# The merges' small products in halves and the queries' norm products in quarters, each part behind a dense tile

## The chip, the core and the metric

One core of one Trainium2 chip runs the whole program. The metric is the device time of one execution in microseconds (us). TensorE is called PE, VectorE DVE, ScalarE ACT, GpSimd POOL, and SyncE SP; SP issues nearly all the loads.

## What is computed

Two blocks on 256 tokens of 1024 features, in float32. The first is a layer with four branches. The second adds 16 meta tokens, runs a mixer and then a mixture of experts. The change lies in the mixer:

```python
def hybrid_mixer(h, norm_g, w_in, conv_w, a_log_f, dt_bias_f, a_log_b, dt_bias_b,
                 out_norm_g, w_fourier, w_delta, w_out):
    hn = rms_norm_2(h, norm_g)
    proj = hn @ w_in
    f_in, qkv, z, ab, gate_f, gate_d = jnp.split(proj, points, axis=-1)
    f_mix = jnp.real(jnp.fft.fft2(fg, axes=(1, 3), norm="ortho")).astype(h.dtype)
    y_f = f_mix.reshape(bsz, seq_len, F_WIDTH) @ w_fourier
    qkv = jax.nn.silu(depthwise_conv_centred(qkv, conv_w))
    q, k, v = jnp.split(qkv, [QK_WIDTH, 2 * QK_WIDTH], axis=-1)
    q = l2_normalize(...) * (HEAD_DK ** -0.5)
    ...
    o_fwd = gated_delta_chunked(qp, kp, vp, pad_to_chunks(g_f), pad_to_chunks(beta_f))
    o_bwd = flip(gated_delta_chunked(flip(qp), ...))
    o = rms_norm_2(o, out_norm_g) * jax.nn.silu(zf)
    y_d = o.reshape(bsz, seq_len, V_WIDTH).astype(h.dtype) @ w_delta
    merged = jax.nn.sigmoid(gate_f) * y_f + jax.nn.sigmoid(gate_d) * y_d
    return merged @ w_out
```

`gated_delta_chunked` solves a unit lower triangular system in each chunk and then scans over the chunks with a state of 128 by 128 for each of 8 heads. The mixture of experts picks one of 8 groups and two of its 8 experts for each token; the kernel reads the weights of all 64 experts, 192 loads of 1 MB, named `wexp`.

## The kernel before

**Dense tiles.** A projection is done in tiles of 128 output features. `load` (L269) has SP fetch the weight tile (`wraw`, L283), ACT writes its high part (`whi`, L293), and POOL or DVE subtracts to get the low part (`wlo`, L300; POOL in two halves). `dense_fm` (L333) then issues 24 PE products per tile: high part by high and low part of the tokens (L340, L341), 8 each, and low part by high part (L345), 8. They have 256 or 272 columns. The tiles of the second block stand in a queue in the order of their weights: among the last are `wf` (the input projections, which the queue takes from first), `wfo` (Fourier output, products with `fhl`), `wde` (delta output) and `wo`.

**Chains woven between dense tiles.** The latency-bound work is written as generators: at each `yield`, `weave` (L973) lets `fill` issue dense tiles, W4 = 1.0 per step for `merges`, W5 = 2.6 per step for `q_factors` and the two scans. The generators' instructions have a raised priority. A list scheduler then fixes the order in which each engine runs its instructions; PE runs what it was given in that order and waits where an operand is not there. So an edit to a generator can move everything behind it.

**merges** (L1455) puts the inverses of 32 diagonal blocks together, from 32 to 64 to 128. First ACT, DVE and POOL copy blocks (L1465, L1467, L1469). `Zp` (L1475) is 64 products of 32 by 32, copied by ACT to `Zs` (L1479); `Wp` (L1485, L1486) is 128 such products. Then `Z2` (L1501) and `W2` (L1511, L1513), two groups of 16 products of 64 by 64 each, with ACT's copies `Z2s` (L1503) between. The two `Z2` and the two `W2` tiles read as `Z` and `W` in the trace.

**q_factors** (L1522) squares the queries on ACT and sums the squares by 16 PE products with one column each (`psrq`, L1529). **scan** (L1546) runs for two directions and two chunks: `psks`, `psqs`, `psvn`, `psS`, and last `pso` (L1605), which DVE adds to the output (`dec`, L1610). When both directions have added theirs, **output_norm** (L1618) squares and sums that output (L1629, L1630), takes a reciprocal root in small DVE steps, scales the output (L1644) and transposes it on PE (`psoT`, L1648). Then `on` (L1671), `hTh` (L1672) and `hTl` (L1674) make the operand of the `wde` tiles; the expert phase comes after those, the output projection and the router.

**Expert loads.** 24 slots hold expert chunks ahead of their use; SP issues the loads into them between the loads of dense tiles. A float32 product shows in the trace as two records.

Of the kernel before, what the change touches and what calls it, by code (L numbers as in the profile page):

```python
# [22 lines left out]
L = NM + S  # L23
# [9 lines left out]
NU = 2  # L33
# [184 lines left out]
def body(ctx, tc, A, out, dbg=None, stage=9):  # L218
    nc = tc.nc
    kit = Kit(tc)  # L220
    V, SC, G, PE = nc.vector, nc.scalar, nc.gpsimd, nc.tensor
# [22 lines left out]
    ones = cp.tile([P, 128], F32, name="ones")  # L244
# [88 lines left out]
    def dense_fm(jobs, x, c0, c1, nk):  # L333

        xh, xl = x
        g = dict(skip_group_check=True) if len(jobs) > 1 else {}
        for j, (ps, (wh, wl), o) in enumerate(jobs):
            for k in range(nk):
                ks = slice(o + k * P, o + k * P + P)
                PE.matmul(ps, wh[:, ks], part(xh, k, slice(c0, c1)), start=j + k == 0, stop=False, **g)  # L340
                PE.matmul(ps, wh[:, ks], part(xl, k, slice(c0, c1)), start=False, stop=False, **g)  # L341
        for j, (ps, (wh, wl), o) in enumerate(jobs):
            for k in range(nk):
                ks = slice(o + k * P, o + k * P + P)
                last = PE.matmul(ps, wl[:, ks], part(xh, k, slice(c0, c1)), start=False, stop=k == nk - 1, **g)  # L345
        return last
# [61 lines left out]
    with ExitStack() as b1:  # L408
# [67 lines left out]
        hT = feature_major(S)  # L476
# [31 lines left out]
        for j in range(4):  # L508
            wst["hi"] = HI0[j]
            w = load(A["wtok"][j], 8 * CH, 2) if j else w0  # L510
# [21 lines left out]
            for t in range(2):  # L532
                ps, rt = pss[t], r1[:, t:t + 1]
# [27 lines left out]
        evac, done = [], []  # L561
# [326 lines left out]
    with b2:  # L888
# [55 lines left out]
        for n in SEQ2:  # L944
            base2[n] = o_
            o_ += (COL2[n][1] - COL2[n][0]) // P
        queue, nload = [], [NU]

        def fill(n=1):
            for _ in range(n):  # L950
# [35 lines left out]
        def dense(n, a, c0, use):  # L986
            def go(w):
                ps = kbig[a] if n == "k" and a in KBIG else bank("psd")
                dense_fm([(ps[:, c0:L], w[0], 0)], hT, c0, L, 8)
                use(a, ps[:, c0:L])  # L990
            queue.append([n, lambda: load_tiles(A["wf2"], base2[n] + a, 1, D), go, None])

# [462 lines left out]
        def merges():  # L1455
# [13 lines left out]
                G.tensor_copy(OTf[bs, :, 32 * (b % 2):32 * (b % 2) + 32],  # L1469
                              src[bs, :, 16 * f:16 * f + 16].rearrange("p c a -> p a c"))  # L1470
            Zp = x32(big("Zp"))
            for a in range(32):
                for p2 in range(2):
                    r0, c0 = 64 * p2, 64 * p2 + 32
                    PE.matmul(Zp[c0:c0 + 32, a], Anf[r0:r0 + 32, a, c0:c0 + 32], Xc[r0:r0 + 32, :, a], start=True, stop=True)  # L1475
            Zs = x32(big_c("Zs"))
            for p2 in range(2):
                c0 = 64 * p2 + 32
                SC.activation(Zs[c0:c0 + 32], Zp[c0:c0 + 32], AF.Copy)  # L1479
            yield  # L1480
            Wp = x32(big("Wp"))
            for a in range(32):
                for p2 in range(2):
                    r0, c0 = 64 * p2, 64 * p2 + 32
                    PE.matmul(Wp[r0:r0 + 32, a], Zs[c0:c0 + 32, a], Xr[c0:c0 + 32, :, a], start=True, stop=True)  # L1485
                    PE.matmul(Wp[c0:c0 + 32, a], Xr[c0:c0 + 32, :, a], Zs[c0:c0 + 32, a], start=True, stop=True)  # L1486
            SC.activation(OTf[32:64, :, 0:32], Wp[32:64, F_], AF.Copy)
            V.tensor_copy(Vff[64:96, F_, 96:128], Wp[64:96, F_])
            SC.activation(Vff[0:32, F_, 32:64], Wp[0:32, F_], AF.Copy)
# [32 lines left out]
        def q_factors():  # L1522
            ps = bank("psrq")
            for t in range(2):
                qsq = big_c("qsq")
                for i, half in enumerate(halves("q")):
                    SC.activation(qsq[:, 4 * i:4 * i + 4], half[:, :, NM + t * P:NM + t * P + P], AF.Square)
                for h in range(8):
                    PE.matmul(ps[:, 8 * t + h:8 * t + h + 1], qsq[:, h], ones[:, 0:1], start=True, stop=True)  # L1529
                yield  # L1530
            V.tensor_scalar(rq, l2(ps[:, :16], 16, "q"), 128 ** -0.5, None, op0=ALU.mult)
            V.tensor_tensor(rq2, rq, rq, op=ALU.mult)

# [525 lines left out]
```

## Time and profile before

| | |
|---|---|
| median of 3 runs | 1168.31 us (1164.94 to 1168.77) |
| profiled execution | 1169.51 us |
| its span | 1167.7 us |
| mean granted TensorE clock | 0.934 |
| PE busy | 1051.7 us, 90% |
| DVE, ACT, POOL busy | 549.8, 440.5, 424.6 us |
| DMA | 307.71 MB, mean 264 GB/s; 420 GB/s in the expert phase |

The span is the profiled execution from its first to its last instruction; the 1.8 us beside it are start and end. "PEclk" is the share of full clock that PE was granted: 1.00 is 2.4 GHz and 0.50 is 1.2 GHz, and a value between is a window that holds both. Busy shares tell which engine works, not which one the end waits for; that is read from what ended the idle time and from the order of the work on PE.

### The profile page before, as it was taken

To read this page: it belongs to the slowest core of one execution; us is meant where nothing else is said; L and a number is where in the kernel's file an instruction comes from. 1 tells how busy PE (TensorE), PEld (TensorE's weight loads), DVE (VectorE), ACT (ScalarE), POOL (GpSimd) and SP (SyncE) were. 2 spreads that over 40 slices of the span, in tenths; PEclk is the share of its full clock that TensorE was granted. 3 is DMA by queue.
4 is the path that set the end of the run, shared out by engine and by line. 5 is a ranking of instruction groups with operands and counts; after the bars stand their busy time and mean duration, and the time that the engine had idled before them with its cause. 6 is when DMAs were issued, how large, how long until landed. Compare 5 with 4: busy or idle time off the path is not lost. (4 is left out here: it accounts for less than half of the span.)

```text
span 1167.7 us, 21453 instructions
## 1 busy us (share of the span) xinstructions
PE 1051.7 (90%) x8798; PEld 849.2 (73%) x8798; DVE 549.8 (47%) x1202; ACT 440.5 (38%) x753; POOL 424.6 (36%) x348
## 2 busy tenths in 40 slices
PE   7999999999998979899999999999977777888794
PEld 7999999999998879799999997455443333443351
DVE  5947754433446798887356874222221111111112
ACT  5546453444457554556323553112111111111112
POOL 4565433567773684869455651000000000000100
PEclk9999998999999989999889999999998898777888
DMA  8554532555554432354228798999999999999994
GB/s 319 178 181 147 179 123 95 196 178 204 181 181 139 148 109 73 109 175 164 74 73 312 288 349 322 408 420 420 420 421 421 420 420 420 421 420 421 420 420 171
DMA packets 58859, 307.71 MB, mean 264 GB/s; under 512 B 5984, under 2 KB 7264, under 8 KB 33280
## 3 DMA queue, kind: packets, MB, share of 16 engines
q1 hardware_dynamic: 56528, 301.59, 66.5%
q10 hardware_dynamic: 2224, 4.65, 1.1%
q8 instruction: 72, 1.18, 0.4%
q14 instruction: 35, 0.29, 0.1%
HBM read 304.12 MB, written 2.10 MB: 262 GB/s over the span
## 5 line engine op out<-in xcount | busy, mean ns | idle before, releaser
L300 POOL TENSOR_TENSOR wlo<-wraw,whi 128x512 fp32r<-128x512 f32 x230 | 322.0, 1424 | 210.0 <-ACT whi L293 135.1
L340 PE MATMUL psd<-hTh,whi 128*128 128x256 f32 (+2 forms) x1096 | 276.8, 289 | 1.4 <-DVE vr L1039 0.6
L341 PE MATMUL psd<-hTl,whi 128*128 128x256 f32 (+2 forms) x1096 | 275.2, 288 | 2.6 <-DVE hTl L458 2.6
L293 ACT ACTIVATE whi<-wraw 128x1024 fp32r<-128x1024 f32 (+1 forms) x183 | 193.8, 1064 | 192.2 <-PE psd L341 143.8
L341 PEld LDWEIGHTS psd<-hTl,whi 128*128 128x128 f32 x1096 | 211.3, 193 | 4.6 <-DVE hTl L458 3.5
L340 PEld LDWEIGHTS psd<-hTh,whi 128*128 128x128 f32 x1096 | 211.6, 193 | 3.8 <-issue 1.5
L1808 PE MATMUL psgu<-wexp,xg 128*32 128x512 f32 x1024 | 146.1, 659 | 39.6 <-DMA wexp<-in_wex_dram 39.4
L345 PE MATMUL psd<-hTh,wlo 128*128 128x256 f32 (+2 forms) x1096 | 157.7, 288 | 0.0
L1996 POOL TENSOR_SCALAR wexp<-cst,gcol 128x128 f32<-128x128 f32 x8 | 4.7, 603 | 389.1 <-PE psgu L1808 389.1
L300 DVE TENSOR_TENSOR wlo<-wraw,whi 128x1024 fp32r<-128x1024 f32 (+1 forms) x68 | 100.9, 1488 | 92.2 <-PE psd L345 52.2
L345 PEld LDWEIGHTS psd<-hTh,wlo 128*128 128x128 f32 x1096 | 143.2, 193 | 1.2 <-issue 1.0
L1808 PEld LDWEIGHTS psgu<-wexp,xg 128*32 128x32 f32 x1024 | 24.8, 112 | 113.2 <-DMA wexp<-in_wex_dram 84.7
L1794 PEld LDWEIGHTS psg<-pm,x 128*128 128x128 f32 x512 | 76.4, 231 | 17.4 <-issue 12.9
L1847 PE MATMUL psy<-wexp,at 128*32 128x256 f32 x1024 | 78.8, 416 | 11.1 <-DVE at L1837 9.2
L1794 PE MATMUL psg<-pm,x 128*128 128x128 f32 x512 | 84.4, 322 | 0.0
L1856 DVE SCALAR_TENSOR_TENSOR yl<-psy,ww,yh 128x256 fp32r<-128x256 f32 x64 | 31.0, 484 | 102.2 <-ACT yh L1855 97.1
L1855 ACT ACTIVATE yh<-psy,ww 128x256 fp32r<-128x256 f32 x64 | 30.3, 474 | 127.4 <-PE psy L1847 121.9
L1814 DVE SCALAR_TENSOR_TENSOR act<-act,psgu 128x256 f32<-128x256 f32 x16 | 6.7, 422 | 132.1 <-ACT act L1813 132.1
L1813 ACT ACTIVATE act<-psgu 128x256 f32<-128x256 f32 x16 | 6.1, 384 | 135.9 <-PE psgu L1808 135.9
L1847 PEld LDWEIGHTS psy<-wexp,at 128*32 128x32 f32 x1024 | 29.6, 114 | 36.9 <-DVE at L1837 13.4
L1796 DVE TENSOR_SCALAR xg<-psg,gcol 128x128 f32<-128x128 f32 x64 | 22.4, 350 | 62.5 <-ACT xg L1795 61.7
L1795 ACT ACTIVATE xg<-psg,gcol 128x128 f32<-128x128 f32 x64 | 23.5, 368 | 71.3 <-PE psg L1794 71.3
(646 smaller groups left out, 1640.1 us busy)
## 6 DMA issues: line engine op xcount, KB each, us to landing
wexp<-in_wex_dram SPq DMA_DIRECT2D x191, 1024.0 KB, 19.8
wraw<-in_wf_dram SPq DMA_DIRECT2D x39, 1024.0 KB, 4.9
wraw<-in_wf_dram SPq DMA_DIRECT2D x53, 512.0 KB, 4.4
wraw<-in_wbr_dram SPq DMA_DIRECT2D x8, 1024.0 KB, 5.2
wraw<-in_wtok_dram SPq DMA_DIRECT2D x4, 1160.0 KB, 8.5
wraw<-in_wout_dram SPq DMA_DIRECT2D x4, 1024.0 KB, 4.7
wraw<-in_wde_dram SPq DMA_DIRECT2D x8, 512.0 KB, 6.2
wraw<-in_wo_dram SPq DMA_DIRECT2D x8, 512.0 KB, 7.2
```

The costliest lines, as they stand in the source:

```text
L293: SC.activation(hi, rs, AF.Copy)
L300: eng.tensor_tensor(lo[:, h], rs[:, h], hi[:, h].bitcast(F32), op=ALU.subtract)
L340: PE.matmul(ps, wh[:, ks], part(xh, k, slice(c0, c1)), start=j + k == 0, stop=False, **g)
L341: PE.matmul(ps, wh[:, ks], part(xl, k, slice(c0, c1)), start=False, stop=False, **g)
L345: last = PE.matmul(ps, wl[:, ks], part(xh, k, slice(c0, c1)), start=False, stop=k == nk - 1, **g)
L1794: PE.matmul(ps[:, f], hn[:, t, fs], self.pm[:, t].rearrange("p e c -> p (e c)"), start=t == 0, stop=t == 1)
L1795: SC.activation(self.xg[:, 2 * f2], ps[:, 0], AF.Copy, scale=gcol[:, 3, 2 * f2:2 * f2 + 1])
L1796: V.tensor_scalar(self.xg[:, 2 * f2 + 1], ps[:, 1], gcol[:, 3, 2 * f2 + 1:2 * f2 + 2], None, op0=ALU.mult)
L1808: PE.matmul(gu[32 * q:32 * q + 32, :], self.xg[:, k, 32 * q:32 * q + 32], ws[k][:, 512 * q:512 * q + 512], start=k == 0, stop=k == 7)
L1847: PE.matmul(self.ps[32 * q:32 * q + 32, cs], self.at[:, k, 32 * q:32 * q + 32], self.ws[8 + c][:, o:o + 256], start=k == 0, stop=k == 1)
L1855: SC.activation(yh, self.ps[:, cs], AF.Copy, scale=self.ww)
L1856: V.scalar_tensor_tensor(yl, self.ps[:, cs], self.ww, yh.bitcast(F32), op0=ALU.mult, op1=ALU.subtract)
```

## The change

`done[0]` keeps the last PE product of the dense tile issued last. `behind_dense()` ties the PE instructions in its block behind that product in PE's order. The `Zp` products, the `Wp` products and each chunk's `psrq` products are split in two, with a `yield` between the parts, so that `weave` issues a dense tile there. The number of instructions is the same.

```diff
-        queue, nload = [], [NU]
+        queue, nload, done = [], [NU], [None]
+
+        def behind_dense():
+
+            return tc.issue_after(done[0].ins)
...
-                dense_fm([(ps[:, c0:L], w[0], 0)], hT, c0, L, 8)
+                done[0] = dense_fm([(ps[:, c0:L], w[0], 0)], hT, c0, L, 8)
...
             Zp = x32(big("Zp"))
-            for a in range(32):
-                for p2 in range(2):
-                    r0, c0 = 64 * p2, 64 * p2 + 32
-                    PE.matmul(Zp[c0:c0 + 32, a], ...)
+            for half in range(2):
+                with behind_dense():
+                    for a in range(16 * half, 16 * half + 16):
+                        for p2 in range(2):
+                            r0, c0 = 64 * p2, 64 * p2 + 32
+                            PE.matmul(Zp[c0:c0 + 32, a], ...)
+                if not half:
+                    yield
...
             Wp = x32(big("Wp"))
-            for a in range(32):
+            for half in range(2):
+                with behind_dense():
+                    for a in range(16 * half, 16 * half + 16):
...
+                if not half:
+                    yield
...
-                for h in range(8):
-                    PE.matmul(ps[:, 8 * t + h:8 * t + h + 1], qsq[:, h], ones[:, 0:1], start=True, stop=True)
-                yield
+                for h0 in (0, 4):
+                    with behind_dense():
+                        for h in range(h0, h0 + 4):
+                            PE.matmul(ps[:, 8 * t + h:8 * t + h + 1], qsq[:, h], ones[:, 0:1], start=True, stop=True)
+                    yield
```

**At the first merge, on PE.** The rows are an engine's instructions in order: line, operation, output and inputs, shape, count. `whi_6225`, `whi_6263` and `wlo_6182` are weight tiles in order of the queue, and `psd` their results. Before:

```order
L341 MATMUL psd_6268<-hTl272_3922,whi_6225 128x256
L345 MATMUL psd_6230<-hTh272_3921,wlo_6182 128x256 x3
L1475 MATMUL Zp_6395<-Xc_6339,An_5385 32x32 x64
L345 MATMUL psd_6230<-hTh272_3921,wlo_6182 128x256 x5
L340 MATMUL psd_6268<-hTh272_3921,whi_6225 128x256
L341 MATMUL psd_6268<-hTl272_3922,whi_6225 128x256
L340 MATMUL psd_6268<-hTh272_3921,whi_6225 128x256
```

After the change, at the same place:

```order
L340 MATMUL psd_6268<-hTh272_3921,whi_6225 128x256
L345 MATMUL psd_6230<-hTh272_3921,wlo_6182 128x256 x4
L341 MATMUL psd_6268<-hTl272_3922,whi_6225 128x256
L340 MATMUL psd_6268<-hTh272_3921,whi_6225 128x256
L341 MATMUL psd_6268<-hTl272_3922,whi_6225 128x256
L340 MATMUL psd_6307<-hTh272_3921,whi_6263 128x256
L341 MATMUL psd_6307<-hTl272_3922,whi_6263 128x256
L340 MATMUL psd_6307<-hTh272_3921,whi_6263 128x256
```

`Zp` has left this place: the products with `whi_6263` now follow the dense products alone: from the four with `wlo_6182` that stood ahead of `Zp`'s old place it is 18 products to the first of them. The first half of `Zp` stands 70 dense products behind that first one, its second half 12 products after that, and the halves of `Wp` come later still with 15 dense products between them.

**At the second merge, on PE.** Before, the first `Z` product group, dense products, the second `Z` group, five dense products, and then:

```order
L340 MATMUL psd<-hTh_3921,whi 128x272
L341 MATMUL psd<-hTl_3922,whi 128x272
L340 MATMUL psd<-hTh_3921,whi 128x272
L341 MATMUL psd<-hTl_3922,whi 128x272
L1511 MATMUL W_6760<-An,Z2s 64x64 x16
L1513 MATMUL W_6778<-Z2s,ofm 64x64 x16
L340 MATMUL psd<-hTh_3921,whi 128x272
```

Now, after 24 dense products that follow the first `Z` group:

```order
L1523 MATMUL W_6799<-An,Z2s 64x64
L1513 MATMUL Z_6768<-An 64x64
L1523 MATMUL W_6799<-An,Z2s 64x64
L1513 MATMUL Z_6768<-An 64x64 x9
L1103 MATMUL psd<-dft,krl 69x128 x2
L1525 MATMUL W_6817<-Z2s,ofm 64x64 x16
L1543 MATMUL psrq<-ones,qsq 128x1 x4
L1111 MATMUL psd<-dft,sy 128x128 x4
L340 MATMUL psd<-hTh_3921,whi 128x256
```

`Z`, `W` and the first quarter of `psrq` now stand in one run; only the two short Fourier products (`dft`) separate the last `Z` from the `W` products that need its copy.

**At the end of the scans, on PE.** Before, the second part of the transposes stands among the `wfo` tiles, 75 of whose products follow it before the first product with `hTh_7558`, which belongs to `wde`:

```order
L341 MATMUL psd<-fhl,whi 128x256
L340 MATMUL psd<-fhl,whi 128x256
L341 MATMUL psd<-fhl,whi 128x256
L340 MATMUL psd<-fhl,whi 128x256
L1648 MATMUL psoT<-cst,dec 128x128 x12
L341 MATMUL psd<-fhl,whi 128x256
L345 MATMUL psd<-fhl,wlo 128x256 x4
L341 MATMUL psd<-fhl,whi 128x256
L345 MATMUL psd<-fhl,wlo 128x256 x4
```

After the change the last `pso` is followed by 48 products of `wfo`, and then:

```order
L341 MATMUL psd<-fhl,whi 128x256
L345 MATMUL psd<-fhl,wlo 128x256 x8
L1662 MATMUL psoT<-cst,dec 128x128 x16
L340 MATMUL psd<-hTh_7558,whi 128x256 x2
L341 MATMUL psd<-hTl_7559,whi 128x256
L340 MATMUL psd<-hTh_7558,whi 128x256
```

All 16 transposes stand behind the last `wfo` product and directly ahead of `wde`. (Before, 55 products of `wfo` and the older tiles and two groups of Fourier products stood between the last `pso` and this second part.)

**At the end of the scans, on DVE.** Before, from the last `vn` to the addition of the last `pso`:

```order
L1580 TENSOR_TENSOR vn<-psvn,be 128x512 x2
L1587 TENSOR_TENSOR oq<-psqs,ex 128x1024
L1630 TENSOR_REDUCE so<-sq 128x4 x2
L1589 TENSOR_TENSOR dec<-dec,oq 128x1024
L1110 TENSOR_TENSOR fhl<-psd,fhl 128x256
L1631 SCALAR_TENSOR_TENSOR so<-so,rq_6382 128x8
L1610 TENSOR_TENSOR dec<-dec,pso 128x512
```

Now:

```order
L1594 TENSOR_TENSOR vn<-psvn,be 128x512 x2
L1601 TENSOR_TENSOR oq<-psqs,ex 128x1024
L1644 TENSOR_REDUCE so<-sq 128x4
L1128 SCALAR_TENSOR_TENSOR mrg_7029<-mrg_7029,psd 128x256
L1644 TENSOR_REDUCE so<-sq 128x4
L1128 SCALAR_TENSOR_TENSOR mrg_7402<-th_6747,psd 128x256
L1128 SCALAR_TENSOR_TENSOR mrg_7417<-th_6861,psd 128x256
L1603 TENSOR_TENSOR dec<-dec,oq 128x1024
L1645 SCALAR_TENSOR_TENSOR so<-so,rq_6382 128x8
L1624 TENSOR_TENSOR dec<-dec,pso 128x512 x2
```

Three `mrg` steps of the `wfo` tiles and two sums of the other chunk's output norm now lie between the last `vn` and the addition of the last `pso`.

## Rows read from the trace of the kernel before

**Rows 1.** Page, part 4: the chain that ended last, share of the span by engine.

```profile
DMA 24%; PE 12%; DVE 1%; ACT 1%; issue 0%; ACTq 0%; SPq 0%
```

**Rows 2.** 10 us windows: length, busy PE, PEld, DVE, ACT, POOL; PEclk, DMA share, GB/s.

```profile
490.00:500.00 10.00, 6.82 (x36) 6.28 (x37) 9.13 (x28) 2.72 (x6) 6.85 (x6) 0.66 0.32 107
...
590.00:600.00 10.00, 10.00 (x62) 10.00 (x62) 7.14 (x23) 2.47 (x3) 6.82 (x11) 0.66 0.03 11
...
720.00:730.00 10.00, 9.49 (x78) 5.58 (x76) 4.51 (x31) 2.25 (x4) 0.00 (x0) 1.00 0.58 223
```

**Rows 3.** The same in 1 us windows, at the first fall of the clock.

```profile
555.00:556.00 1.00, 1.00 (x79) 1.00 (x71) 0.00 (x0) 0.00 (x0) 0.00 (x0) 1.00 0.73 131
557.00:558.00 1.00, 1.00 (x22) 0.94 (x23) 0.00 (x0) 0.38 (x1) 0.00 (x0) 0.50 0.70 176
```

**Rows 4.** Timeline of PE, first merge (start us, us, line, operation, count, idle before).

```profile
543.91 0.52 PE L345 MATMUL psd<-hTh,wlo 128*128 128x256 f32 x3
544.36 3.80 PE L1475 MATMUL Zp<-Xc,An 32*32 32x32 f32 x128
...
551.72 0.22 PE L1485 MATMUL Wp<-Xr,Zs 32*32 32x32 f32 x1
```

**Rows 5.** Timeline of PE behind it, to the second merge.

```profile
557.52 1.22 PE L345 MATMUL psd<-hTh,wlo 128*128 128x256 f32 x4
558.54 0.43 PE L340 MATMUL psd<-hTh,whi 128*128 128x272 f32 x1
558.76 0.43 PE L341 MATMUL psd<-hTl,whi 128*128 128x272 f32 x1
...
562.51 2.24 PE L1501 MATMUL Z<-ofm,An 64*64 64x64 f32 x32
...
564.91 0.29 PE L341 MATMUL psd<-hTl,whi 128*128 128x272 f32 x1
565.03 0.29 PE L340 MATMUL psd<-hTh,whi 128*128 128x272 f32 x1
```

**Rows 6.** Timeline of PE at the queries' norm products.

```profile
587.29 4.15 PE L1529 MATMUL psrq<-ones,qsq 128*128 128x1 f32 x32
591.30 0.56 PE L341 MATMUL psd<-hTl,whi 128*128 128x256 f32 x1
...
596.35 0.63 PE L1099 MATMUL psd<-dft,krl 128*69 128x128 f32 x2
```

**Rows 7.** Timeline of ACT at the merges.

```profile
541.53 4.49 ACT L1465 ACTIVATE An<-Xr 32x512 f32<-32x512 f32 x4 [0.54 <-DVE Xr L1415]
...
547.10 1.06 ACT L293 ACTIVATE whi<-wraw 128x1024 fp32r<-128x1024 f32 x1
...
568.12 1.02 ACT L1503 ACTIVATE Z2s<-Z 64x1024 f32<-64x1024 f32 x1 [2.31 <-PE Z L1501]
```

**Rows 8.** Timeline of PE from the last scan product to the first wde product.

```profile
639.68 1.95 PE L1605 MATMUL pso<-vn,qk 128*128 128x128 f32 x16
...
649.57 0.38 PE L340 MATMUL psd<-fhl,whi 128*128 128x256 f32 x1 [1.44 <-ACT mrg L1117]
...
651.91 1.47 PE L1648 MATMUL psoT<-cst,dec 128*128 128x128 f32 x12
...
662.49 0.28 PE L340 MATMUL psd<-hTh,whi 128*128 128x256 f32 x1
```

**Rows 9.** Timeline of DVE in the same stretch.

```profile
637.35 1.21 DVE L1587 TENSOR_TENSOR oq<-psqs,ex 128x1024 f32<-128x1024 f32 x1
...
641.67 0.69 DVE L1610 TENSOR_TENSOR dec<-dec,pso 128x512 f32<-128x512 f32 x1
...
647.86 4.66 DVE L1644 TENSOR_TENSOR dec<-dec,ro 128x512 f32<-128x512 f32 x4
...
652.77 1.40 DVE L1671 SCALAR_TENSOR_TENSOR on<-psoT,prm,sz 128x512 f32<-128x512 f32 x2
```

**Rows 10.** Timeline of POOL in the same stretch.

```profile
647.90 3.46 POOL L300 TENSOR_TENSOR wlo<-wraw,whi 128x512 fp32r<-128x512 f32 x2 [2.18 <-ACT whi L293]
```

More of the change, by code (lines that the diff above doesn't have):

```diff
@@ L1471, in merges @@
             Zp = x32(big("Zp"))
-            for a in range(32):
-                for p2 in range(2):
-                    r0, c0 = 64 * p2, 64 * p2 + 32
-                    PE.matmul(Zp[c0:c0 + 32, a], Anf[r0:r0 + 32, a, c0:c0 + 32], Xc[r0:r0 + 32, :, a], start=True, stop=True)
+            for half in range(2):
[3 more added lines that the diff above has]
+                            r0, c0 = 64 * p2, 64 * p2 + 32
+                            PE.matmul(Zp[c0:c0 + 32, a], Anf[r0:r0 + 32, a, c0:c0 + 32], Xc[r0:r0 + 32, :, a], start=True, stop=True)
+                if not half:
+                    yield
             Zs = x32(big_c("Zs"))
@@ L1481, in merges @@
             Wp = x32(big("Wp"))
-            for a in range(32):
[L1483 to L1486, printed above, removed]
+            for half in range(2):
+                with behind_dense():
+                    for a in range(16 * half, 16 * half + 16):
+                        for p2 in range(2):
+                            r0, c0 = 64 * p2, 64 * p2 + 32
+                            PE.matmul(Wp[r0:r0 + 32, a], Zs[c0:c0 + 32, a], Xr[c0:c0 + 32, :, a], start=True, stop=True)
+                            PE.matmul(Wp[c0:c0 + 32, a], Xr[c0:c0 + 32, :, a], Zs[c0:c0 + 32, a], start=True, stop=True)
+                if not half:
+                    yield
             SC.activation(OTf[32:64, :, 0:32], Wp[32:64, F_], AF.Copy)
```

## The prediction

> **What bounds the kernel now.** I read the end first. The chain that ended last spends 24% of the span on the experts' loads and half of that on PE [rows 1]: the experts run at the pace of the DMA. The DMA is not behind when they begin, though: at 720 to 730 us it is busy for only 0.58 of the time [rows 2], as the 24 slots are full and the next load waits for the first expert. So every microsecond by which the dense part ends earlier or later moves the end by one.
>
> Then I read the stretch that the change touches, 540 to 663 us. PE is busy there in nearly all windows, so what counts is the pace of PE and the few places where it waits. The pace falls twice. In the window 555 to 556 the clock is 1.00, in 557 to 558 it is 0.50, with PE busy 1.00 in both [rows 3]; ahead of the fall PE had run `Wp`'s 32 by 32 products since 551.72 [rows 4]. The window 590 to 600 has 0.66 [rows 2], and ahead of it PE ran 32 `psrq` records from 587.29 [rows 6]. Dense products start 0.226 apart at the low clock (558.54, 558.76) and 0.12 at full (564.91, 565.03) [rows 5]. `Zp`, 3.80 us of equally small products [rows 4], lowered nothing, nor did `Z` after 562.51 [rows 5].
>
> The only wait of PE in the last part is 1.44 us at 649.57 [rows 8].
>
> **The change part by part.** I sum against the profiled execution, 1169.51 us, which is 1.2 above the median of the runs shown.
>
> *The two falls of the clock.* From 557.52 to 562.51 PE does 21 dense products in 4.99 us [rows 5]; at 0.12 to 0.126 they take 2.6, so 2.4 goes to the clock. From 591.30 to 596.35 it does 23 in 5.05 us [rows 6]; at 0.12 they take 2.8: 2.2. With the small products on both sides of each, some 0.6 more: 5.2 in all. The change cuts `Wp` into two parts of about 2.5 us with 15 dense products (1.9 us) between them, and `psrq` into four parts of 1.0 us with over 7 us of other work between. Each part is shorter than the 3.80 us of `Zp` that cost nothing. I take both falls as gone: **-5.2** (bounds -5.2 and 0).
>
> *What `Zp` covered.* ACT does four copies L1465 from 541.53 for 4.49 us, and only at 547.10 to 548.16 the high part `whi_6263` [rows 7]. Before, PE had `Zp` to do in that time. Now the first product with `whi_6263` stands 18 products behind 543.91 [rows 4], at 543.91 + 18 x 0.12 = 546.1; ACT's order is as before, so PE waits till 548.16: 2.0. The next tiles follow at once and need ACT's copy and POOL's two subtractions (2.5 us and more per tile against PE's 2.9), which started as late; I add 1.0 for them. `Zp`'s own time is only moved. **+3.0** (bounds 1.0, if ACT's copies come earlier, and 4.0).
>
> *The second merge.* The last `Z` product is followed by ACT's copy of 1.02 us (568.12 in [rows 7]), and the second half of `W` needs it. Before, five dense products and the first half of `W`, about 1.9 us, lay between. Now two Fourier products do, some 0.4: **+0.7** (0 to 1.2). `Z`, `W`, this wait and four `psrq` products now make some 9 us with almost no dense work. The rows show no fall in the `Z` and `W` stretch, but 11 dense products and more lay in that; a fall here costs at most what one cost before, 2.6. I take 0 and keep 2.6 for the range.
>
> *The end of the scans.* This is the large term. The `wde` tiles need `hTh` and `hTl`, these need the transposes, these the scaled output, and that the last `pso`. Before, 21 us lay between `pso` (over at 641.6) and the first `wde` product at 662.49 [rows 8], all filled with dense products but for 1.44. Now 48 products, 5.8 us, stand there. The chain, step by step: DVE starts adding `pso` late, as it first has `oq` (1.21 [rows 9]), two reductions and three `mrg` steps (by columns 0.6 and 0.3 each, estimates from the `oq` row) and the addition of `oq` (1.2) to do; 4.5 in all, of which PE's `pso` and the products ahead of it cover some 2.5: 2.0 late. From that addition to the scaling L1644 it was 647.86 - 641.67 = 6.2 [rows 9]; four more `mrg` steps now stand in that, less one `fhl`: 6.8. Three of the four scalings must be done before the first transpose: 3 x 0.6 = 1.8 if free, 3/4 of 4.66 = 3.5 as they ran [rows 9]; 2.4. Together 11.2 after `pso`, less 5.8 of products: PE waits 5.4. Then the transposes, 1.6 (12 records took 1.47 [rows 8]), while DVE does the fourth scaling (0.6), a low part of a weight tile that stands in its queue (1.2), `on` (1.40 for two halves [rows 9]), two `hTl` (1.2), half of the next `on` (0.7), and ACT the copy (0.6): 5.6 from the first transpose to the first `wde` product, 4.0 of it idle. The last `hTl` holds the next products by 0.4. Sum 9.8, less the 1.44 that this takes in: **+8.4** (bounds 6 with free scalings and the `mrg` steps not in the way, 11 at the old pace of the scalings). Behind all this DVE serves nobody else: PE has no other tile left in its order.
>
> The old pace is itself to be explained. POOL subtracted from 647.90 for 3.46 us [rows 10], and DVE's scalings took 4.66 for four in the same time [rows 9], where one addition of the same shape took 0.69. The Trainium skill, "SBUF — State Buffer", section "Who interferes with whom", says that DVE and GpSimd share one pair of ports and that an operation holds it as an exclusive lock. The row agrees; by that rule the term is near 8.4 if POOL is again subtracting then, and near 7 if it is done.
>
> *The clock after that wait.* In the window 490 to 500 PE is busy for only 6.82 of 10 us, and the clock is 0.66 [rows 2]. The new waits are longer, so `wde` starts at the low clock: 15 to 30 products at 0.1 each, **+2.0** (0 to 3.4).
>
> *What is not on the path.* SP now issues the first loads of `wfo` ahead of four expert loads. The DMA has 0.03 to do at 590 to 600 [rows 2], which covers that; a chunk that came late would cost 1 MB at the 420 GB/s of the table, 2.5. The scans' steps move 10 to 15 us later between the same dense products; what they wait for (DVE, ACT) has time there as before: 0.
>
> Sum: -5.2 + 3.0 + 0.7 + 8.4 + 2.0 = +8.9, or 1178.4 in the profiled execution's terms, and **1177.2** beside the median.
>
> **The rivals.** *The scans' end is covered* (faster): if the chain behind the last `pso` takes under 6 us more than the dense products ahead of the transposes, its wait stays near the old 1.44 and no new fall follows. That decides the sign: with +3.7 from the merges and -5.2, and ACT ahead by a little, it is 1168.3 - 5.2 + 1.0 = 1164. Against it stands the order, in which `wde` has nothing ahead of it but the transposes.
>
> *The losses come out at their lower ends* (no change): -5.2 + 1.0 + 0 + 6 + 0 = +1.8, 1170.
>
> *The falls of the clock stay*, or come back elsewhere (slower still): the dense part between two halves is only 1.9 us, and the long run of `Z` and `W` is new. Without the gain it is 1177.2 + 5.2 = 1182.4, with one new fall 1179.8. For it: PE counts as busy in full in [rows 3] while the clock falls, so busy time does not tell what holds the clock. The Trainium skill, "TensorE: Matmul & The Clock Gate", section "What's actually happening", has the clock follow how busy PE has been; by that rule taken with the profile's busy share, small products would not lower it, cutting them would change nothing, and the time would be that of this rival. The trace speaks against the busy share as its measure.
>
> **How the numbers follow.** The forecast, with both falls gone and the wait at the end of the scans, has 0.62 (1174 to 1181). The falls staying or a new one has 0.16 (1179 to 1187). The low ends have 0.13 (1166 to 1171), and the covered end 0.09 (1160 to 1165). A measurement can tell about 0.3%, 3.5 us, from no change. So faster 0.09, same 0.13, slower 0.78. The range from 1168 to 1185 leaves out the covered end, half of the low ends and a little at the top.
>
> **What would show it.** In the trace after: PEclk 1.00 through `Wp` and `psrq`; PE idle some 2 us ahead of the products with `whi_6263`, released by ACT L293; an idle time under 1.5 us ahead of the second half of `W`, released by ACT; PE idle for 5 us ahead of the transposes, released by DVE's scaling L1658, and for 4 us ahead of the first `wde` product, released by `hTh`; a window at 0.5 after that. The first expert products come about 9 us later, and the end with them. If the end moves by less than the experts' start, the DMA had room that I have not seen. If the transposes find `dec` ready, the large term is wrong, and with it the sign.

## The result and the profile after

The change makes the kernel slower: 1183.87 us in the median (1182.25 to 1187.87, 4 runs) against 1168.30 (1164.94 to 1168.77, 4 runs), a ratio of 1.0122 with a 95% interval from 1.0095 to 1.0148 (the two medians alone give 1.0133). The profiled execution took 1187.87 us, its span is 1186.0 us; before, 1169.51 and 1167.7. So the traces are 18.4 us apart where the medians are 15.6 apart, and the account below has to say where the other 3 come from.

First the windows of the changed kernel (window: length, busy PE, PEld, DVE, ACT, POOL; PEclk, DMA share, GB/s):

```profile
540.00:550.00 10.00, 7.86 (x56) 6.70 (x56) 9.12 (x7) 8.40 (x10) 9.73 (x9) 1.00 0.39 141
550.00:560.00 10.00, 10.00 (x78) 9.85 (x79) 1.53 (x4) 4.11 (x7) 9.64 (x9) 0.83 0.28 105
570.00:580.00 10.00, 9.81 (x296) 9.23 (x295) 2.68 (x10) 3.52 (x6) 6.14 (x13) 1.00 0.23 70
590.00:600.00 10.00, 10.00 (x102) 9.93 (x100) 3.49 (x5) 3.07 (x7) 2.68 (x2) 1.00 0.22 86
660.00:670.00 10.00, 3.68 (x16) 3.28 (x16) 7.86 (x20) 2.38 (x3) 3.60 (x3) 0.67 0.45 184
670.00:680.00 10.00, 6.47 (x40) 6.25 (x41) 5.29 (x10) 3.58 (x5) 1.11 (x3) 0.65 0.75 278
```

They answer to [rows 2, 3]. The stretches with `Wp` (570 to 580) and with the first `psrq` products (590 to 600) now have a clock of 1.00: the two falls are gone. (A fall is a stretch in which the granted clock is 0.50; before, these were 556.1 to 562.9 and 590.2 to 597.0.) In their place PE idles 2.1 us in 540 to 550, the clock is 0.83 in 550 to 560, and from 660 to 680 PE is busy for only half of the time, at 0.67 and 0.65. The new falls are 550.7 to 554.1 and 663.3 to 677.0.

PE's timeline at the place where `Zp` stood (start us, us, engine, line, operation, count; idle before and what ended it):

```profile
545.32 0.64 PE L345 MATMUL psd<-hTh,wlo 128*128 128x256 f32 x4
...
549.76 0.39 PE L340 MATMUL psd<-hTh,whi 128*128 128x256 f32 x1 [2.14 <-ACT whi L293]
...
559.76 1.98 PE L1481 MATMUL Zp<-Xc,An 32*32 32x32 f32 x64
```

and ACT's at the same time:

```profile
542.95 4.63 ACT L1469 ACTIVATE An<-Xr 32x512 f32<-32x512 f32 x4 [0.56 <-DVE Xr L1419]
547.60 1.02 ACT L1454 ACTIVATE krl<-pS 128x1024 f32<-128x1024 f32 x1
548.65 1.06 ACT L293 ACTIVATE whi<-wraw 128x1024 fp32r<-128x1024 f32 x1
```

The first row is the one at 543.91 of [rows 4]; it comes 1.4 us later although PE's order up to here is the same in both traces, record for record; 1.3 of it is there already within the first 52 us. That is one execution against another. From this row on PE does 18 dense products and then waits 2.14 us for the high part that ACT finishes at 549.71, after its four copies and the copy `krl`, as in [rows 7]. From 550.71 on the dense products are 0.21 apart, until 554.24: behind this wait the clock fell. (The same wait was followed by a fall in e1 and e9 below, and by none in e7.) `Zp` starts at 559.76 instead of 544.36.

The second merge, PE again:

```profile
576.41 0.21 PE L1495 MATMUL Wp<-Xr,Zs 32*32 32x32 f32 x1 [0.19 <-issue]
...
589.42 2.08 PE L1525 MATMUL W<-Z2s,ofm 64*64 64x64 f32 x32 [0.52 <-ACT Z2s L1515]
```

A gap of 0.19 inside `Wp` (0.68 before), and 0.52 for the copy `Z2s`. No fall of the clock follows.

The end of the scans, PE:

```profile
650.80 1.95 PE L1619 MATMUL pso<-vn,qk 128*128 128x128 f32 x16
...
657.39 1.11 PE L345 MATMUL psd<-fhl,wlo 128*128 128x256 f32 x8
665.64 3.68 PE L1662 MATMUL psoT<-cst,dec 128*128 128x128 f32 x16 [7.14 <-DVE dec L1658]
673.52 0.79 PE L340 MATMUL psd<-hTh,whi 128*128 128x256 f32 x2 [4.21 <-ACT hTh L1686]
```

DVE in the same stretch:

```profile
649.82 1.22 DVE L1601 TENSOR_TENSOR oq<-psqs,ex 128x1024 f32<-128x1024 f32 x1
...
653.12 1.58 DVE L1603 TENSOR_TENSOR dec<-dec,oq 128x1024 f32<-128x1024 f32 x1
...
655.79 1.27 DVE L1624 TENSOR_TENSOR dec<-dec,pso 128x512 f32<-128x512 f32 x2
...
661.35 2.36 DVE L1658 TENSOR_TENSOR dec<-dec,ro 128x512 f32<-128x512 f32 x2
663.64 1.22 DVE L1656 TENSOR_TENSOR ro<-ro,rq 128x8 f32<-128x8 f32 x1
664.89 1.29 DVE L1658 TENSOR_TENSOR dec<-dec,ro 128x512 f32<-128x512 f32 x2
...
669.35 1.41 DVE L1685 SCALAR_TENSOR_TENSOR on<-psoT,prm,sz 128x512 f32<-128x512 f32 x2 [2.03 <-PE psoT L1662]
```

and POOL:

```profile
661.40 3.43 POOL L300 TENSOR_TENSOR wlo<-wraw,whi 128x512 fp32r<-128x512 f32 x2 [4.30 <-ACT whi L293]
```

These answer to [rows 8, 9, 10]. Behind the last `pso` PE does its 48 `wfo` products until 658.5 and then waits 7.14 us for the scaling L1658; the transposes take 3.68 us, as the clock has fallen to 0.50 in the wait (each now lasts 0.421 instead of 0.272, and they overlap); and PE waits another 4.21 us for `hTh`. DVE adds the last `pso` at 655.79 because it first had `oq`, the sums, three `mrg` steps and the addition of `oq` to do. While POOL subtracts from 661.40 to 664.83, two scalings take 2.36 us and a step on 8 elements per lane (663.64) takes 1.22, where such steps take 0.17 with POOL idle; it ends at 664.86, with POOL's second subtraction. The next two scalings, behind POOL's end, take 1.29.

Last, SP's queue (the loads, in order). Before, from its end:

```profile
689.26 0.81 SPq L283 DMA_DIRECT2D wraw<-in_wo_dram  x2
695.30 0.33 SPq L913 DMA_DIRECT2D wexp<-in_wex_dram  x1
```

After the change:

```profile
690.91 4.86 SPq L283 DMA_DIRECT2D wraw<-in_wo_dram  x4
698.82 5.33 SPq L913 DMA_DIRECT2D wexp<-in_wex_dram  x2
704.27 5.80 SPq L283 DMA_DIRECT2D wraw<-in_wo_dram  x4
```

Before, the four pairs of `wo` loads stood one by one between single expert loads. Now the last four wait behind two expert loads. PE then has four waits, 1.6 us in all, between 700 and 715, where it had none:

```profile
701.34 0.74 PE L365 MATMUL psd<-wlo,mxmrg 128*128 128x256 f32 x4 [0.45 <-POOL wlo L300]
703.76 0.50 PE L360 MATMUL psd<-whi,mxsgd 128*128 128x256 f32 x2 [0.50 <-DVE mxsgd L324]
712.35 0.38 PE L359 MATMUL psd<-whi,mxmrg 128*128 128x256 f32 x1 [0.48 <-ACT whi L293]
```

With the fourth, 0.16 for POOL's low part, three of them, 1.1 us, are for parts of `wo` weights; the one of 0.50 is for a step of DVE and is not shown to come from the loads.

So from one trace to the other:

| where | us |
|---|---|
| start of the stretch, nothing moved ahead of it | +1.4 |
| wait for the high part behind the old place of `Zp` | +2.1 |
| fall of the clock behind that wait (8 + 8 products and some more at 0.21) | +1.6 |
| falls behind `Wp` and `psrq` gone (5.2, worked out from the rows before), with the smaller gap in `Wp` | -5.7 |
| wait for `Z2s` | +0.5 |
| waits at the end of the scans, 7.14 + 4.21 - 1.44 | +9.9 |
| the transposes at the low clock, 3.7 - 1.6 | +2.1 |
| first `wde` products at the low clock | +1.6 |
| waits between 700 and 715 (1.1 of them for `wo` weights) | +1.6 |
| last expert at the low clock, this execution | +3.4 |

The sum is 18.5 of 18.4; single steps are good to some 0.9, by which the pieces up to the first `wde` product (11.9) miss the 11.0 that lie between 662.49 and 673.52. The expert phase begins (first `pspos`) at 735.70 instead of 720.75, 15.0 later, near the 15.6 between the medians. A second count bears the table out: from 540 us to the first `pspos` PE is idle for 16.7 us instead of 3.1, and runs at the low clock for 17.1 us instead of 13.7. So the clock that the change won behind `Wp` and `psrq` it lost again elsewhere, and the idle time, 13.5 us more, is with the 1.4 at the start the whole of the 15.0.

The last row of the table is no part of the change: e1 below begins its experts at 735.73 and ends 3.7 us earlier. In the changed kernel's trace the clock is low from 1158.3 to 1168.5, while the last expert runs; so it is for some time near the end in e5, e6 and e10, and in no other trace. From the first `pspos` to the end these four take 448.6 to 450.3 us, the others 446.1 to 448.1. A window at the last expert, the changed kernel first and then e1:

```profile
1160.00:1165.00 5.00, 4.56 (x34) 2.19 (x27) 0.48 (x1) 0.53 (x2) 0.00 (x0) 0.50 0.53 215
```

```profile
1160.00:1165.00 5.00, 4.21 (x46) 2.43 (x44) 1.64 (x4) 1.96 (x8) 0.00 (x0) 1.00 0.44 179
```

### The profile page after: what moved, and what is told of

Its sections match the earlier page's. It is cut to its first block, busy times and chain, and to the rows that moved or that the text cites. A ratio compares the mean times of both kernels' runs of the same rounds, so it can differ in the third digit from the quotient of the medians.

```text
span 1186.0 us, 21460 instructions
## 1 busy us (share of the span) xinstructions
PE 1054.7 (89%) x8798; PEld 850.0 (72%) x8798; DVE 543.7 (46%) x1202; ACT 438.4 (37%) x751; POOL 417.4 (35%) x348
## 4 chain that ended last, share of the span: by engine, by line
PE 53%; DMA 24%; DVE 9%; ACT 2%; issue 2%; POOL 1%; ACTq 0%; SPq 0%; POOLq 0%; DVEq 0%
DMA wexp<-in_wex_dram 23%; PE psd L340 10%; PE psd L341 10%; PE psd L345 10%; PE psg L1808 3%; PE psy L1861 3%; PE psgu L1822 3%; PE acc L1875 1%; DVE ofm L1040 1%; PE psd L359 1%; PE psd L360 1%; PE psd L365 1%; DVE An L1320 1%; PE psvn L1588 1%; DMA wraw<-in_wo_dram 1%
## 5 line engine op out<-in xcount | busy, mean ns | idle before, releaser
L300 POOL TENSOR_TENSOR wlo<-wraw,whi 128x512 fp32r<-128x512 f32 x230 | 316.0, 1397 | 207.9 <-ACT whi L293 122.7
L1822 PE MATMUL psgu<-wexp,xg 128*32 128x512 f32 x1024 | 143.5, 650 | 41.2 <-DMA wexp<-in_wex_dram 41.1
L300 DVE TENSOR_TENSOR wlo<-wraw,whi 128x1024 fp32r<-128x1024 f32 (+1 forms) x68 | 98.5, 1452 | 93.3 <-PE psd L345 52.9
L1861 PE MATMUL psy<-wexp,at 128*32 128x256 f32 x1024 | 81.6, 428 | 10.7 <-DVE at L1851 9.2
L1861 PEld LDWEIGHTS psy<-wexp,at 128*32 128x32 f32 x1024 | 30.1, 116 | 38.3 <-DVE at L1851 13.5
```

Source lines behind the costliest of these rows:

```text
L300: eng.tensor_tensor(lo[:, h], rs[:, h], hi[:, h].bitcast(F32), op=ALU.subtract)
L1822: PE.matmul(gu[32 * q:32 * q + 32, :], self.xg[:, k, 32 * q:32 * q + 32], ws[k][:, 512 * q:512 * q + 512], start=k == 0, stop=k == 7)
L1861: PE.matmul(self.ps[32 * q:32 * q + 32, cs], self.at[:, k, 32 * q:32 * q + 32], self.ws[8 + c][:, o:o + 256], start=k == 0, stop=k == 1)
```

## The experiments

The theory, formed with the trace of after in hand, is called M in what follows: the tie puts the products behind the *newest* dense tile in the program, which PE does 83 dense products later than the place where the products could have run; everything that hangs on the merges (second merge, scans, output norm, `wde`) starts that much later, and at the end there is no dense work left to cover it. Q: it is the norm products' tie that holds the scans back. Y: the additional yields alone do it. The table holds what the traces show of each kernel; the change is the second line. Each ratio is against the kernel before, run beside it. The times are those of one execution each, and executions of one kernel differ by up to 11 us (e3: 1166.33 to 1177.68); "left" is the number of dense products in PE's order between the last `pso` and the first `wde` product, which is fixed by the program and the same in every execution.

| kernel | ratio (95% interval) | first `Wp` | last `pso` | left | experts begin | falls of the clock behind `Wp` / `psrq` |
|---|---|---|---|---|---|---|
| before | 1 | 551.7 | 641.4 | 130 | 720.7 | yes / yes |
| the change | 1.0122 (1.0095 to 1.0148) | 569.0 | 652.5 | 48 | 735.7 | no / no |
| e1 merges only | 1.0124 (1.0084 to 1.0164) | 567.8 | 656.0 | 24 | 735.7 | no / yes |
| e2 norm products only | 1.0023 (0.9999 to 1.0048) | 553.1 | 651.0 | 72 | 728.5 | yes / no |
| e3 cuts without tie | 0.9998 (0.9970 to 1.0026) | 556.8 | 648.7 | 114 | 727.2 | yes / yes |
| e4 earlier tiles | 0.9961 (0.9941 to 0.9981) | 553.3 | 637.6 | 120 | 719.1 | no / no |
| e5 e4 with `Wp` uncut | 1.0108 (1.0077 to 1.0138) | 551.8 | 648.4 | 98 | 728.3 | yes / no |
| e6 e4 with `psrq` uncut | 1.0005 (0.9984 to 1.0026) | 550.9 | 640.2 | 120 | 720.8 | no / yes |
| e7 tie two tiles back | 1.0126 (1.0087 to 1.0164) | 565.2 | 652.5 | 64 | 734.7 | yes / no |
| e8 e4 with W5 = 2.2 | 0.9984 (0.9962 to 1.0007) | 552.0 | 636.4 | 120 | 717.7 | no / no |
| e9 tie without cuts | 1.0157 (1.0131 to 1.0183) | 564.3 | 653.0 | 58 | 736.0 | yes / yes |
| e10 e4 again | 0.9978 (0.9963 to 0.9993) | 550.8 | 635.0 | 120 | 716.9 | no / no |

**e1, the merges alone.** The norm products go back to 8 per chunk:

```diff
-                for h0 in (0, 4):
-                    with behind_dense():
-                        for h in range(h0, h0 + 4):
-                            PE.matmul(ps[:, 8 * t + h:8 * t + h + 1], ...)
-                    yield
+                for h in range(8):
+                    PE.matmul(ps[:, 8 * t + h:8 * t + h + 1], ...)
+                yield
```

> Only the merges' products are cut and tied; the queries' norm products are as before (8 per chunk, no tie). Theory M (the tie moves the first merge behind dense tiles that PE does 83 products later, so the scans end late and their end has no dense products beside it): PE waits some 2 us for the high part of a weight tile (ACT L293) near 548, and over 10 us in all ahead of the transposes and of the first wde product; time 1178 to 1186 us, close to the full change. Theory Q (the norm products' tie holds the scans back, as their squares keep buffers that the scans want): the wait at the end is near the old 1.44 us; time 1165 to 1172.

Measured: 1184.98 us, as the full change. PE waits 2.14 us for the high part and, at the end of the scans:

```profile
665.37 3.66 PE L1660 MATMUL psoT<-cst,dec 128*128 128x128 f32 x16 [6.20 <-DVE dec L1656]
673.24 0.79 PE L340 MATMUL psd<-hTh,whi 128*128 128x256 f32 x2 [4.21 <-ACT hTh L1684]
```

6.20 + 4.21 against 7.14 + 4.21. So the merges' part alone makes a loss as large as that of the change, and Q is not needed for it.

**e2, the norm products alone.** `Zp` and `Wp` as before, `psrq` as in the change.

> Only the queries' norm products are cut and tied; the merges are as before. Theory M: no wait near 548, the fall of the clock behind Wp stays, the one behind the norm products goes (-2.5 us), and the end of the scans is as before: 1164 to 1168 us. Theory Q: the scans' last pso comes later by some 10 us, PE waits 4 to 8 us ahead of the transposes, which still have 48 dense products behind them; 1169 to 1177 us.

Measured: 1174.16 us, 3.4 above the kernel before on the same chip, though the interval just holds 1. That is in the range written for Q and not in M's. The fall behind `psrq` is gone, as M said (window 590 to 600), but the scans end late, as Q said: the last `pso` is 9.6 us later and PE waits 5.43 us ahead of the transposes, which still have 48 dense products behind them. So with the norm products' tie alone the scans end late too, at a price of 3.4 us that is just not clear of noise.

```profile
540.00:550.00 10.00, 10.00 (x165) 9.36 (x164) 7.61 (x8) 9.25 (x10) 9.68 (x9) 0.79 0.36 110
560.00:570.00 10.00, 10.00 (x97) 9.49 (x95) 2.07 (x3) 3.85 (x5) 0.00 (x0) 0.68 0.01 2
590.00:600.00 10.00, 10.00 (x90) 10.00 (x90) 9.62 (x13) 4.05 (x7) 10.00 (x16) 1.00 0.31 107
```

```profile
659.58 3.67 PE L1654 MATMUL psoT<-cst,dec 128*128 128x128 f32 x16 [5.43 <-DVE dec L1650]
```

The windows from 540 and from 560 show two falls where the kernel before had one in this stretch: `Zp`, in the same order as before, saw the clock fall here (545.8 to 552.7) and did not in the trace of before; behind `Wp` it fell at 559.5, and PE stood idle in `Wp` for 2.34 us. So part of the late `pso` is the clock. That the scans' buffers are held by the squares is what the expectation said; no run shows it.

**e3, the cuts without the tie.**

```diff
-            return tc.issue_after(done[0].ins)
+            return ExitStack()
```

> All cuts and all yields of the change, without the tie behind a dense tile. In PE's order Zp, Wp and the 16 norm products then each stand in one run again. If the tie is what costs (M or Q): both falls of the clock are there as before, no wait at the first merge, and the time is that of the kernel before within 3 us, 1166 to 1172 us. If the two more yields of the merges cost (they let two more dense tiles ahead of the scans): PE waits over 5 us at the end of the scans, 1174 to 1182 us.

Measured: 1169.46 us, no difference (0.9998); the profiled execution was some 6 us longer than this median, which must be kept in mind with its line of the table. Without the tie the scheduler puts the halves together again, and the falls are there:

```profile
550.00:560.00 10.00, 10.00 (x273) 9.63 (x270) 3.09 (x4) 5.95 (x8) 8.03 (x8) 0.83 0.15 43
560.00:570.00 10.00, 7.60 (x147) 7.29 (x140) 2.07 (x3) 2.82 (x4) 0.00 (x0) 0.66 0.26 100
610.00:620.00 10.00, 10.00 (x78) 10.00 (x78) 7.77 (x19) 5.28 (x7) 4.40 (x3) 0.87 0.50 163
```

(551.1 to 554.5 at `Zp`, 561.3 to 568.1 at `Wp`, 609.1 to 612.5 behind `psrq`.) So the yields alone cost nothing that can be measured, and cuts alone change nothing: Y falls.

**e9, the tie without the cuts.**

```diff
-            for half in range(2):
-                with behind_dense():
-                    for a in range(16 * half, 16 * half + 16):
...
-                if not half:
-                    yield
+            with behind_dense():
+                    for a in range(32):
```

and the same for `Wp` and for the 8 norm products of a chunk.

> The tie alone: Zp, Wp and the norm products uncut, without the new yields, each behind the newest dense tile. Theory M: Zp stands 83 dense products later as in the full change, the first Z product 137 products behind Zp's old place instead of 167, so PE waits 2 us for the high part near 548 and 8 to 11 us at the end of the scans; 1178 to 1186 us. If tie and cuts are needed together for the loss: 1166 to 1173 us. The clock should fall behind Wp, as it is in one run.

Measured: 1188.26 us, above the range written for M and no less than the full change.

```profile
666.36 3.30 PE L1655 MATMUL psoT<-cst,dec 128*128 128x128 f32 x16 [6.08 <-DVE dec L1651]
673.87 0.80 PE L340 MATMUL psd<-hTh,whi 128*128 128x256 f32 x2 [4.21 <-ACT hTh L1679]
```

```profile
560.00:570.00 10.00, 9.50 (x284) 9.05 (x283) 0.65 (x4) 3.77 (x5) 4.03 (x8) 0.83 0.32 111
570.00:580.00 10.00, 10.00 (x104) 9.45 (x97) 2.72 (x7) 5.48 (x8) 4.83 (x8) 0.83 0.01 2
```

The waits of 6.08 and 4.21 us are there without any cut, and falls behind `Zp` and `Wp` too. With e3 this separates the two halves of the change: the tie makes the loss. That the cuts give back some of it (1.0157 against 1.0122) is not shown, as the two intervals overlap.

**e7, a tie two tiles further back**, with all cuts of the change:

```diff
-            return tc.issue_after(done[0].ins)
+            return tc.issue_after(done[-1 - 2].ins)
...
-                done[0] = dense_fm([(ps[:, c0:L], w[0], 0)], hT, c0, L, 8)
+                last = dense_fm([(ps[:, c0:L], w[0], 0)], hT, c0, L, 8)
+                done.append(last)
```

> All cuts of the change, but each part tied behind the third last dense tile. The first part of Zp then stands 39 dense products later than before instead of 83, the first Z product behind 142 instead of 167 (before: 52). If the loss follows from how late the merge comes (theory M): a smaller loss at the end of the scans than the full change, 6 to 9 us of wait instead of 11.3, and 1175 to 1182 us. If it does not depend on how late: 1183 to 1186 us as the full change, or 1168 as before.

Measured: 1184.01 us, as much as the full change, and the waits are

```profile
665.02 3.68 PE L1663 MATMUL psoT<-cst,dec 128*128 128x128 f32 x16 [4.59 <-DVE dec L1659]
673.86 0.80 PE L340 MATMUL psd<-hTh,whi 128*128 128x256 f32 x2 [5.16 <-ACT hTh L1687]
```

4.59 + 5.16 = 9.8 instead of 11.3. The smaller loss that M was to bring did not come, and the time lies where it was expected if the loss does not depend on how late the merge comes. Against reading it so: the wait is smaller by 1.6, and a fall of the clock behind `Wp` came back, whose halves stand in one run here. The first `Wp` is only 3.8 us earlier than in the change, and 64 dense products are left behind the last `pso` against 48, so the dose was too small to tell by the time.

**e4, the tie behind tiles that PE has nearly reached.** `Zp` uncut and untied, the halves of `Wp` behind the fifth last dense tile, the parts of the norm products behind the third last:

```diff
-        def behind_dense():
+        def behind_dense(back):
 
-            return tc.issue_after(done[0].ins)
+            return tc.issue_after(done[-1 - back].ins)
...
-                with behind_dense():
+                with behind_dense(4):
...
-                    with behind_dense():
+                    with behind_dense(2):
```

> Zp in one run; the halves of Wp tied behind the fifth last dense tile instead of the last, the parts of the norm products behind the third last. 8 dense products then stand between the halves of Wp, and the merge is not moved. If the tie behind the newest tile is the cause of the losses and cutting does hold the clock: no wait near 548, at most one fall of the clock, PE's wait at the end of the scans under 4 us, 1160 to 1168 us. If 8 products between the halves are too few to hold the clock: a fall behind Wp as before, 1166 to 1171 us. If the scans' end is late from the yields alone: over 1172 us.

Measured: 1167.17 us, 0.9961, faster than the kernel before.

```profile
550.00:560.00 10.00, 10.00 (x298) 9.47 (x298) 1.27 (x3) 5.07 (x8) 8.25 (x8) 1.00 0.30 104
590.00:600.00 10.00, 10.00 (x90) 10.00 (x90) 8.48 (x14) 2.71 (x5) 5.52 (x9) 1.00 0.30 107
```

```profile
646.30 0.45 PE L340 MATMUL psd<-fhl,whi 128*128 128x256 f32 x1 [3.57 <-ACT mrg L1122]
...
651.86 0.60 PE L1659 MATMUL psoT<-cst,dec 128*128 128x128 f32 x4
```

With eight dense products between the halves of `Wp`, and the norm products in runs of 16, 8 and 8 records instead of one of 32, the clock is 1.00 in both windows. The first `Wp` is near where it was before, and the transposes find `dec` ready. What is left is 3.57 us of wait at 646.30, for ACT's `mrg`, ahead of which ACT's timeline has two table loads of 1.28 us, for the reciprocal root and back; the wait at 649.57 in [rows 8] is the same, with 1.44. Behind the wait of 3.57 the clock falls, from 646.5 to 649.9, the only fall between 540 us and the experts.

**e10, e4 again with more rounds.**

> e4 once more, with more rounds. If its gain is one of the kernel: a ratio of 0.994 to 0.998 and again no fall of the clock behind Wp and the norm products. If it was one of that run: 0.999 to 1.002.

Measured: 1167.72 us, 0.9978 (0.9963 to 0.9993). The gain repeats in sign, at about half of its size; both intervals lie under 1.

Neither `Wp` nor the parts of `psrq` are followed by a fall in its trace; the experts begin at 716.9.

**e5, `Wp` uncut again** (the block of the kernel before in place of the two halves; the norm products as in e4).

> As e4, but Wp in one run again; only the norm products are cut, each part behind the third last dense tile. If cutting Wp is worth something by the clock: a fall of the clock behind Wp as before, 1168 to 1172 us, some 2 to 3 us above e4. If e4's gain came from the norm products alone: 1164 to 1168 us.

Measured: 1181.9 us, which no expectation had. The fall behind `Wp` is back:

```profile
550.00:560.00 10.00, 9.05 (x284) 8.55 (x283) 1.11 (x2) 3.93 (x6) 4.26 (x5) 0.81 0.35 108
```

but the order of the scans also came out otherwise: PE waits 2.69 us for a state ahead of a `pso`, and at the end of the scans 6.0 us in four waits (1.07, 1.91, 1.35 and 1.64), with 98 dense products left:

```profile
618.16 3.44 PE L1612 MATMUL pso<-vn,qk 128*128 128x128 f32 x16 [2.69 <-DVE krl L1609]
```

So e5 says nothing clean of what cutting `Wp` is worth. It shows that one edit to a generator moves the whole list behind it, and that 1.1% can be lost with merges that are not moved and a tie to an earlier tile.

**e6, `psrq` uncut again** (16 products, no tie; `Wp` as in e4).

> As e4, but the 16 norm products in one run and untied. If cutting them is worth something by the clock: a fall behind them as before, 1168 to 1172 us. If e4's gain came from Wp alone: 1164 to 1168 us. If neither part matters and e4 gained by another order alone: both e5 and e6 stay within 1 us of e4.

Measured: 1170.83 us, no difference to the kernel before, against 0.9961 and 0.9978 for e4 and e10. The fall is back at `psrq` (586.2 to 593.0) and not behind `Wp`. That this fall alone makes the difference is not shown: e6 also waits otherwise at the end of the scans (1.19, 1.20 and 0.91 us in place of e4's 3.57), and its interval overlaps that of e10.

```profile
550.00:560.00 10.00, 10.00 (x298) 9.32 (x297) 2.22 (x4) 3.80 (x7) 5.90 (x6) 1.00 0.36 108
580.00:590.00 10.00, 10.00 (x73) 9.82 (x72) 9.49 (x15) 2.96 (x5) 9.29 (x12) 0.81 0.43 163
```

**e8, e4 with W5 = 2.2.**

> e4 with W5 = 2.2 instead of 2.6, so that the scans let fewer dense tiles between their steps. The last pso then has 71 dense products between it and the transposes and 49 behind them. If e4's 3.6 us of wait at the end is a matter of these two stretches: the wait goes under 2 us, 1163 to 1166 us. If not: as e4, 1166 to 1169 us.

Measured: 1167.54 us, 0.9984 (0.9962 to 1.0007): like e4, not better. The wait is smaller,

```profile
644.27 0.39 PE L340 MATMUL psd<-fhl,whi 128*128 128x256 f32 x1 [2.25 <-ACT mrg L1122]
```

and another of 1.58 us for `hTl` has come.

**What the runs say together.** Wherever the merges are tied to the newest tile or to the third last (the change, e1, e7, e9), the first `Wp` comes 12.6 to 17.3 us later than before and the experts begin 14 to 15 us later; wherever they are not (e2 to e6, e8, e10), the first `Wp` is within 6 us of before, and the experts begin between 3.8 us earlier and 7.8 us later.

The column "left" says how the place of the merges reaches the end. Between the `pS` products ahead of the merges and the first `wde` product, PE has 452 dense products to do in each of the kernels. The change puts 83 more of them ahead of `Zp`, and 82 fewer are left behind the last `pso`, 48 instead of 130. The kernels that lose nothing (e3, e4, e6, e8, e10) have 114 to 120 left, those that lose 1% or more 24 to 98, and e2, whose interval just holds 1, has 72. So the count goes with the loss, though not in proportion: e1 with 24 loses no more than the change with 48.

Cutting does go with a clock that holds: `Wp` in one run saw a fall in 6 of 6 traces, `Wp` with 8 or 15 dense products in its middle in 0 of 6. Each of the six uncut runs also has an idle gap in it (0.50 to 2.58 us). The gap cannot have brought the fall where the fall began first (556.07 against 556.33 before, 556.29 against 556.44 in e5; in e3 they begin within 0.03); in e2, e7 and e9 the gap came first, and its part is open. The 32 records of `psrq` in one run have no gap and saw a fall in 3 of 3 (before, e3, e6); a run of 16 records saw one in e1 and e9 and none in e4, e5, e7, e8 and e10.

## Why the prediction was right, and where it was too small

The sign and the range were right, the size was not: +8.9 us was forecast, +15.6 came. The time of 1183.87 lies above the 1174 to 1181 that the forecast gave for its own case, in the stretch that it kept for falls of the clock that stay or come anew. By the table of traces, without the 1.4 at the start and the 3.4 of the last expert, 13.7 us are explained against the forecast's 8.9; the rest up to 15.6 is within what executions and single steps differ by.

*The falls of the clock*: as forecast, the two are gone, and there is no new one in the run of `Z` and `W`. What that is worth, 5.2, is worked out from the rows before and measured by no run alone.

*What `Zp` covered*: 2.0 forecast, 2.14 measured, at the place and from the releaser named. The further 1.0 for the next tiles did not come as a wait; a fall of the clock of 1.6 came, which I had not in the sum: I priced a wait of 2 us by its length alone.

*The second merge*: 0.7 forecast, 0.52 measured.

*The end of the scans*: the mechanism was right and the term was mis-sized, +8.4 against +9.9. The transposes wait for the scaling (5.4 forecast, 7.14 measured), `wde` for `hTh` (4.0 and 4.21). Of the three steps ahead of the transposes, two were too small and one too large. DVE reached the addition of `pso` 3.0 us after PE's last `pso` record had ended (650.80 + 1.95), not 2.0. From there to the scalings it took 5.6, not 6.8 (7.1 by the forecast's own prices, as four `mrg` steps are 1.2 and the `fhl` taken off is 0.3). From the first scaling to the first transpose it took 4.3, not 2.4, nor the 3.5 of the old pace: POOL was subtracting beside DVE, and a small step of 1.22, which takes 0.17 otherwise, stood among the scalings. The Trainium skill, "SBUF — State Buffer", section "Who interferes with whom", has the ports that DVE and GpSimd share held as an exclusive lock. The trace agrees: the small step ends at 664.86 and POOL's second subtraction at 664.83.

*The clock after the wait*: +2.0 forecast for `wde`, 1.6 measured, but the transposes in the middle of the wait ran at the low clock as well, +2.1, and were not in the sum.

*What is not on the path*: this step failed. I set the loads' order at nothing by looking at the DMA at 590 to 600 us; the order that cost was that of the `wo` loads a hundred microseconds later, 1.1 of the 1.6 us of waits there (e7, which loses as much, has none of them). And I put the scans' move "10 to 15 us later" down at nothing.

*The reason behind the large term* was told too narrowly. I took the 48 products at the end as given and built the term from DVE's queue behind the last `pso`. The runs e1, e3 and e9 show that the cause lies at the front: with the tie on the merges the loss is there, without the tie it is not, and the cuts are not needed for it. The tie starts the merges 15 us later; the 83 dense products that PE does meanwhile are those that are missing behind the last `pso`.

*The rivals*: the covered end did not come. (Its 1164 takes the merges at +1.0; with the +3.7 named beside it, it would have been 1166.8.) Of the rival of the falls, the first half did not come, and the second half did: new falls came at 550.7 and 663.3, both with waits. In [rows 3] the clock fell with PE's busy share at 1.00, and with cut `Wp` it held at the same share (550 to 560 in e4), which speaks against the busy share as the clock's measure, as I had argued.

## What to carry to other kernels

When products are tied behind other work to fill a gap, ask which instruction the tie names and when the engine does that one: the newest in the program may be many microseconds behind in the engine's order, and what is tied is often the head of the longest chain. Tying to a tile that the engine has nearly reached kept a gain, of 0.2 to 0.4%, and lost the cost (e4, e10), though the same tie on the norm products alone lost 1.1% by another order of the scans (e5): count, in the new order, how much filling work is left behind the chain's last step. And a wait on PE is priced with the clock that it may take away from the work behind it, not by its length alone: of the nine waits of 2.1 to 3.6 us that PE had outside `Wp` between 540 us and the experts (one each in the change, e1, e3, e4, e5 and e7 to e10), seven went with a fall, and two did not (2.18 in e7, 2.17 in e3).

## What was not expected of the hardware

The clock at the same run of small products is not the same in each execution. `Zp`, 3.8 us of 32 by 32 products in the same place, with PE's order ahead of it the same record for record, saw a fall in e2 (545.8 to 552.7) and e3 (551.1 to 554.5) and none in the traces of before, e4, e5, e6, e8 and e10. Likewise the changed kernel's last expert ran at 0.50 from 1158.3 to 1168.5 and e1's at 1.00, in two kernels whose experts began at the same time and whose ends are 3.7 us apart.

PE can also stop inside a run of small products with nothing in the trace that it waits for, always inside `Wp`: in its uncut runs 0.68 us before, 2.34 in e2, 2.40 in e3, 0.95 in e5, 2.58 in e7 and 0.50 in e9, in its cut ones 0.19 in the changed kernel, 0.35 in e1 and none in the others. What it waits for there is open.
